# One of four weight sums is added up by an accumulating DMA instead of VectorE

## The chip, the core and the metric

The kernel runs on one core of a Trainium2 chip. The metric is the device time of one execution in microseconds (us). Its engines are TensorE (PE in the profile; PEld is its weight load), VectorE (DVE), ScalarE (ACT), GpSimd (POOL) and SyncE (SP, which here only issues DMAs).

## The reference

Two transformer layers over 512 frames of 1024 features, all in float32. The first mixes by multi-head latent attention with a chunk mask, the second by chunked attention with a learned relative bias. Each is followed by the same feed-forward network with its own weights, 1024 to 2816 to 1024, with norms before and behind:

```python
def swiglu(h, w_gate, w_up, w_down):
    return (jax.nn.silu(h @ w_gate) * (h @ w_up)) @ w_down
...
h = rms_norm(x, ffn_pre_g[layer])
f = swiglu(h, ffn_w_gate[layer], ffn_w_up[layer], ffn_w_down[layer])
x = x + rms_norm(f, ffn_post_g[layer])
```

The change lies in `h @ w_gate` and `h @ w_up` of both layers.

## The kernel before

Features lie on the partitions, frames on the free dimension. A float32 product is made of three products of rounded pieces: each operand is split into a high piece (a rounding copy on ACT, L141) and a low piece (what is left, a subtraction on DVE, L142), and high x high, high x low and low x high are added up in PSUM. So each weight tile of 128 x 1024 is loaded by SP (`raw`), cast on ACT (`whi`), subtracted on DVE (`wlo`), and then used by PE.

The hidden layer has 22 blocks of 128. The first four are computed whole. The other 18 are computed in 9 pairs per layer by `products`: the weights of a pair (gate and up of two blocks, with the input features in two halves) are cut into quarters, and seven products of half the size take the place of eight, in the manner of Strassen and Winograd. For that, sums of weight quarters are needed, and sums of input quarters, which `blocks_of` makes once per layer (`t`, with pieces `th` and `tl`, L1016 to L1019, partly on POOL). In each pair PE runs the products 0 to 6 one after the other, 24 multiplications of 256 columns a product (L1053), in the banks `be`, `al`, `ga`. Between them DVE and ACT take partial results out of the banks (`gt`, `ut`, L1057 to L1072), and at the end of a pair DVE and ACT form the gated hidden block and its pieces (`hh`, `hl`).

The quarters of a pair are four tiles in DRAM, `src[0]` to `src[3]`, here tile(0) to tile(3). `Pair` loads them into `raw[1]`, `raw[2]`, `raw[4]` and `raw[5]` of its dictionary, and product j uses `raw[j]`:

- product 0: `raw[0]` = tile(2) + tile(3), in a tile of its own
- product 1: tile(0); product 2: tile(1)
- product 3: `raw[0]` + tile(0), written over `raw[0]`
- product 4, the fifth: tile(2) + tile(0), written over `raw[4]`
- product 5: tile(3)
- product 6: `raw[3]` + tile(1), written over it once more

All four sums are DVE instructions of one line, L171. tile(2) has a ring of two buffers of its own (`sum2`), the sum `raw[0]` has another (`sum`), and the other three quarters share a ring of four buffers (`raw`) in which later loads wait until an earlier tile has been read for the last time. All loads are issued by SP in one queue.

`Feed` walks a plan of all weight tiles: it loads ahead (up to five steps within pairs), and `split(i)` calls `sums(j)` and then splits the tile. The framework puts every engine's instructions in order ahead of time, by a priority that follows the program and by when it reckons an instruction's inputs to be ready; each engine then works its queue strictly in that order, and an instruction that waits holds up what stands behind it. In this way the sums are put well ahead of their use: the first sum of a pair stands in DVE's queue more than a pair before its product.

Of the kernel before, what the change touches and what calls it, by code (L numbers as in the profile page):

```python
# [14 lines left out]
OP = mybir.AluOpType  # L15
# [53 lines left out]
def trunk(ctx: ExitStack, tc: tile.TileContext, a, out):  # L69
    nc = tc.nc  # L70
# [11 lines left out]
    def name_(n):  # L82
        uid[0] += 1
        return f"{n}_{uid[0]}"
# [63 lines left out]
    class Pair:  # L148

        def __init__(self, src):
            self.src, self.raw = src, {}

# [13 lines left out]
        def sums(self, j):  # L169
            def plus(t, x, y):  # L170
                V.tensor_tensor(t, x, y, op=OP.add)  # L171

            r = self.raw
            if j == 0:
                r[0] = r[3] = r[6] = wide[0].tile([P, 1024], F32, tag="sum", name=name_("raw"), bufs=2)
                plus(r[0], r[4], r[5])
            elif j in (3, 6):
                plus(r[j], r[j], r[j // 3])
            elif j == 4:
                plus(r[4], r[4], r[1])  # L180

    wide = [None]

# [198 lines left out]
    class Head:  # L382
# [3 lines left out]
        def __init__(self, qk, bt, scale, pv, sums):  # L386
            self.qk, self.bt, self.scale, self.pv, self.sums = qk, bt, scale, pv, sums
            self.p, self.pt = {}, None
# [493 lines left out]
    def start_a(h):  # L882
# [12 lines left out]
        def pv(pth, ptl):  # L895
            fill.until("v")
            o = bank()
            v_ = slice(h * VD, (h + 1) * VD)
            for kt in range(NQT):
                q_ = slice(kt * P, S)  # L900
                mm3(o[:, q_], (va[kt][:, 0, v_], va[kt][:, 1, v_]), (pth[:, kt, q_], ptl[:, kt, q_]),
                    kt == 0, kt == NQT - 1)
            V.reciprocal(sums, sums)
            of = U(name="of")
            nc.scalar.copy(of, o)

            def rest():
                V.tensor_tensor(of, of, spread(sums), op=OP.mult)
                oh, ol = U(F32R, "oh"), U(F32R, "ol")
                split(oh, ol, of)  # L910
                osp.append((oh, ol))

            return rest
# [415 lines left out]
```

## Time and profile before

| what | value |
|---|---|
| time, median of 3 runs | 1172.71 us |
| the three runs | 1174.03, 1170.98, 1172.71 us |
| the profiled execution: time | 1172.07 us |
| the profiled execution: span from first to last instruction | 1170.3 us |
| mean granted TensorE clock over the span | 0.992 |
| the seven products, first layer | about 237 to 428 us from the span's start |
| the seven products, second layer | about 847 to 1038 us |

A row of a timeline gives the start in us from the span's start, the length in us, the engine, the line, the operation and its operands (out<-in, buffer numbers left out), how many instructions were merged into the row, and in brackets how long the engine sat idle before it and what ended that. A row of the chain of waits gives start, length and what: an instruction of an engine, a DMA in flight, or "issue", in which the engine waited for nothing that the profile shows. Lengths on an engine can overlap by some 0.1 us, so the cost of one instruction in a full queue is better read from start to start.

### The profile page before, as it was taken

The numbers are of one execution on the slowest core, as the hardware profiler recorded it, in microseconds if no ns is written. First come the engines' busy times: TensorE is split into PE (matmuls) and PEld (weight loads), VectorE is DVE, ScalarE is ACT, GpSimd is POOL, SyncE is SP. The second block draws the span as 40 slices with busy tenths as digits, with TensorE's granted clock in tenths as the row PEclk, the third lists the DMA queues.
The fourth block names the chain that finished last, engine by engine and source line by source line (L and its number), as shares of the span: only waits on it lengthen the run. The fifth ranks groups of instructions, "written<-read, shape, count | busy, mean of one in ns | idle before, by whom it ended". The sixth has DMA issues, their size and how long they took to land.

```text
span 1170.3 us, 18693 instructions
## 1 busy us (share of the span) xinstructions
PE 1142.9 (98%) x7195; PEld 1023.0 (87%) x7195; DVE 832.5 (71%) x1405; ACT 611.4 (52%) x1151; POOL 45.6 (4%) x67
## 2 busy tenths in 40 slices
PE   9999999989999999999999999999989999999996
PEld 6888889889999998889788887789889999998886
DVE  7787648889889862236968877749899898952233
ACT  6476546556556552234436766656555565642220
POOL 0200000110000000000100000000300000000002
PEclk9999999989999999999999999999999999999998
DMA  7433144222323243233546656454123233252222
GB/s 215 118 105 91 37 163 153 99 73 91 127 90 106 85 141 129 93 113 100 179 145 156 172 150 171 118 198 142 57 91 114 85 94 123 73 175 95 99 63 73
DMA packets 53161, 137.71 MB, mean 118 GB/s; under 512 B 7184, under 2 KB 10768, under 8 KB 53072
## 3 DMA queue, kind: packets, MB, share of 16 engines
q1 hardware_dynamic: 52928, 136.47, 37.5%
q8 instruction: 57, 0.93, 0.3%
q14 instruction: 32, 0.26, 0.1%
q10 hardware_dynamic: 144, 0.04, 0.0%
HBM read 113.22 MB, written 8.59 MB: 104 GB/s over the span
## 4 chain that ended last, share of the span: by engine, by line
PE 76%; DVE 13%; DMA 4%; issue 3%; ACT 2%; POOL 1%; SPq 0%; DVEq 0%; ACTq 0%; POOLq 0%
PE b L258 16%; PE b L259 16%; PE b L260 16%; PE al L1053 12%; PE be L1053 6%; DVE wlo L142 5%; PE ga L1053 3%; DMA raw<-in_w_pair 2%; PE pt L410 2%; DVE raw L171 2%; DVE tl L142 1%; PE sc L1170 1%; PE b L1179 1%; PE bc L371 1%; PE b L1178 1%
## 5 line engine op out<-in xcount | busy, mean ns | idle before, releaser
L141 ACT CAST whi<-raw 128x1024 fp32r<-128x1024 f32 (+4 forms) x240 | 240.5, 1002 | 324.8 <-PE b L259 172.4
L142 DVE TENSOR_TENSOR wlo<-raw,whi 128x1024 fp32r<-128x1024 f32 (+4 forms) x240 | 279.8, 1168 | 167.5 <-ACT whi L141 162.2
L258 PE MATMUL b<-hh,whi 128*128 128x512 f32 (+1 forms) x364 | 136.0, 374 | 0.0
L259 PE MATMUL b<-hl,whi 128*128 128x512 f32 (+1 forms) x364 | 135.7, 373 | 0.0
L260 PE MATMUL b<-hh,wlo 128*128 128x512 f32 (+1 forms) x364 | 135.6, 373 | 0.0
L1053 PE MATMUL al<-th,whi 128*128 128x256 f32 x432 | 124.5, 288 | 2.8 <-DVE ut L1065 2.6
L1053 PE MATMUL al<-tl,whi 128*128 128x256 f32 x432 | 122.1, 283 | 0.0
L1053 PE MATMUL al<-th,wlo 128*128 128x256 f32 x432 | 122.1, 283 | 0.0
L258 PE MATMUL b<-xh,whi 128*128 128x512 f32 (+1 forms) x304 | 115.8, 383 | 1.5 <-ACT xh L145 1.5
L259 PE MATMUL b<-xl,whi 128*128 128x512 f32 (+1 forms) x304 | 113.0, 372 | 0.0
L260 PE MATMUL b<-xh,wlo 128*128 128x512 f32 (+1 forms) x304 | 112.8, 371 | 0.0
L171 DVE TENSOR_TENSOR raw<-raw,raw 128x1024 f32<-128x1024 f32 x72 | 88.1, 1225 | 24.1 <-DMA raw<-in_w_pair 23.6
L1053 PEld LDWEIGHTS al<-th,whi 128*128 128x128 f32 x432 | 82.6, 191 | 5.8 <-DVE ut L1065 4.2
L1053 PEld LDWEIGHTS al<-tl,whi 128*128 128x128 f32 x432 | 82.7, 192 | 0.0
L1053 PEld LDWEIGHTS al<-th,wlo 128*128 128x128 f32 x432 | 82.7, 191 | 0.0
L258 PEld LDWEIGHTS b<-hh,whi 128*128 128x128 f32 x364 | 68.5, 188 | 12.1
L260 PEld LDWEIGHTS b<-hh,wlo 128*128 128x128 f32 x364 | 68.5, 188 | 11.9
L259 PEld LDWEIGHTS b<-hl,whi 128*128 128x128 f32 x364 | 68.5, 188 | 11.9
L398 ACT ACTIVATE p<-p,mn 128x128 f32<-128x128 f32 (+1 forms) x96 | 54.0, 563 | 34.8 <-DVE mn L396 34.2
L328 DVE TENSOR_TENSOR acc<-acc,sq 128x256 f32<-128x256 f32 (+1 forms) x89 | 43.7, 504 | 35.1 <-ACT sq L327 33.1
L142 DVE TENSOR_TENSOR ptl<-pt,pth 128x128 fp32r<-128x128 f32 (+1 forms) x96 | 46.4, 485 | 28.6 <-ACT pth L141 21.9
L258 PEld LDWEIGHTS b<-xh,whi 128*128 128x128 f32 x304 | 57.5, 190 | 9.7 <-ACT xh L145 2.8
(265 smaller groups left out, 2852.7 us busy)
## 6 DMA issues: line engine op xcount, KB each, us to landing
raw<-in_w_pair SPq DMA_DIRECT2D x72, 512.0 KB, 3.6
raw<-in_w_down SPq DMA_DIRECT2D x38, 512.0 KB, 3.4
raw<-in_w_o SPq DMA_DIRECT2D x16, 512.0 KB, 3.6
raw<-in_w_gu SPq DMA_DIRECT2D x16, 512.0 KB, 4.3
raw<-in_w_qkb SPq DMA_DIRECT2D x16, 512.0 KB, 3.9
x<-in_x SPq DMA_DIRECT2D x16, 256.0 KB, 5.9
mid<-x SPq DMA_DIRECT2D x16, 256.0 KB, 2.2
x<-mid SPq DMA_DIRECT2D x16, 256.0 KB, 6.0
```

The lines of the kernel that those rows point to most:

```text
L141: return (nc.scalar.copy(dst_hi, src), V.tensor_tensor(dst_lo, src, dst_hi.bitcast(F32), op=OP.subtract))
L142: V.tensor_tensor(dst_lo, src, dst_hi.bitcast(F32), op=OP.subtract))
L171: V.tensor_tensor(t, x, y, op=OP.add)
L258: nc.tensor.matmul(o, l[0], r[0], start=start, stop=False)
L259: nc.tensor.matmul(o, l[0], r[1], start=False, stop=False)
L260: nc.tensor.matmul(o, l[1], r[0], start=False, stop=stop)
L328: V.tensor_tensor(self.acc[:, c], self.acc[:, c], q[:, c], op=OP.add)
L371: nc.tensor.transpose(b[:, (first + i) * P:(first + i + 1) * P], col[:, i:i + 1].to_broadcast([P, P]), ident)
L398: nc.scalar.activation(p[:, :n], p[:, :n], AF.Exp, bias=mn[:, :1], scale=-1.0, accum_out=self.sums[:, qt:qt + 1])
L410: nc.tensor.transpose(t[:, kt * P:(kt + 1) * P], p[:, kt * P:(kt + 1) * P], ident)
L1053: nc.tensor.matmul(o, l[c], r[d], start=first_ and n == 0, stop=k == K2 - 1 and n == 2, skip_group_check=True)
L1170: nc.tensor.matmul(o, q1[:, e, q_], k1[:, e, :n], start=True, stop=False)
```

## The change

`sums(0)` still adds tile(2) and tile(3) on VectorE. Behind that it issues a DMA on POOL's queue that reads tile(0) from DRAM again and adds it to `raw[4]`, the tile in which tile(2) lies. The VectorE sum for product 4 goes. The sums for products 0, 3 and 6 stay, and tile(0) is still loaded into `raw[1]`. What casts `raw[4]` for product 4 now waits for that DMA. A blank line is added above, so that the line of the sums becomes L172; lines from L181 on keep their numbers.

```diff
@@ -150,6 +150,7 @@
+
         def __init__(self, src):
             self.src, self.raw = src, {}
...
             if j == 0:
                 r[0] = r[3] = r[6] = wide[0].tile([P, 1024], F32, tag="sum", name=name_("raw"), bufs=2)
                 plus(r[0], r[4], r[5])
+                nc.gpsimd.dma_start(r[4], self.src[0], accum_op=OP.add)
             elif j in (3, 6):
                 plus(r[j], r[j], r[j // 3])
-            elif j == 4:
-                plus(r[4], r[4], r[1])
```

## The prediction

> **What bounds the kernel now.** I read the page first, then the product stage by stretches, then the chain of waits inside it, then the engines' timelines around one turn of that chain. On the page, the busy shares and the one group that the change touches:
>
> ```profile
> span 1170.3 us, 18693 instructions
> PE 1142.9 (98%) x7195; PEld 1023.0 (87%) x7195; DVE 832.5 (71%) x1405; ACT 611.4 (52%) x1151; POOL 45.6 (4%) x67
> L171 DVE TENSOR_TENSOR raw<-raw,raw 128x1024 f32<-128x1024 f32 x72 | 88.1, 1225 | 24.1 <-DMA raw<-in_w_pair 23.6
> ```
>
> TensorE is busy nearly all the time, so removed VectorE time counts only where TensorE waits for VectorE. The 72 sums of weight quarters (four in each of 18 pairs) take 88.1 us of VectorE, and VectorE stood idle 23.6 us before some of them until a load had landed. The stretches (columns: length, then busy time of PE, PEld, DVE, ACT, POOL, granted clock, DMA share, GB/s) show where that matters:
>
> ```profile
> 237.00:264.00 27.00, 23.86 (x171) 22.95 (x170) 24.00 (x31) 14.36 (x24) 2.42 (x2) 0.87 0.24 79
> 305.00:367.00 62.00, 61.01 (x501) 60.11 (x500) 54.76 (x70) 35.19 (x57) 0.00 (x0) 1.00 0.32 103
> 847.00:873.00 26.00, 22.57 (x171) 21.83 (x171) 24.04 (x31) 14.26 (x24) 2.43 (x2) 0.93 0.25 82
> 873.00:934.00 61.00, 61.00 (x507) 60.70 (x506) 54.06 (x69) 35.58 (x57) 0.00 (x0) 1.00 0.33 104
> 934.00:1018.00 84.00, 82.21 (x674) 80.99 (x673) 74.09 (x95) 47.09 (x76) 0.00 (x0) 1.00 0.30 95
> ```
>
> From 873 to 934 TensorE is never idle; from 305 to 367 and from 934 to 1018 it is. The chain of waits (start, length, what) says how long a pair of hidden blocks takes in either regime:
>
> ```profile
> 272.96 8.79 PE al L1053 x72
> ...
> 293.27 8.79 PE al L1053 x72
> 302.05 2.90 PE be L1053 x24
> ...
> 364.72 1.32 PE be L1053 x11
> 931.31 5.76 PE be L1053 x48
> ...
> 968.53 4.36 DMA raw<-in_w_pair
> ...
> 989.55 4.50 DMA raw<-in_w_pair
> ...
> 1015.33 4.68 PE be L1053 x39
> ```
>
> Where TensorE is the bound, a pair takes 293.27 - 272.96 = 20.31 us. From the seventh product at 302.05 to that at 364.72 there are three pairs: 62.67 us, 1.74 more than 3 x 20.31. From 931.31 to 1015.33 there are four: 84.02 us, 2.78 more than 81.24. In these stretches the chain leaves TensorE and turns in a loop of VectorE work and one load, 989.55 - 968.53 = 21.02 us a turn. One turn on VectorE's timeline, what TensorE's product line waited for in the whole run (us, times), and in the last row what the sums' line waited for:
>
> ```profile
> 965.50 0.74 DVE L1061 TENSOR_TENSOR gt<-gt,ga 128x256 f32<-128x256 f32 x2
> 966.16 1.22 DVE L171 TENSOR_TENSOR raw<-raw,raw 128x1024 f32<-128x1024 f32 x1
> 967.29 2.35 DVE L142 TENSOR_TENSOR wlo<-raw,whi 128x1024 fp32r<-128x1024 f32 x2
> 969.56 0.74 DVE L1065 TENSOR_TENSOR ut<-al,ut 128x256 f32<-128x256 f32 x2
> 973.02 1.23 DVE L171 TENSOR_TENSOR raw<-raw,raw 128x1024 f32<-128x1024 f32 x1 [2.71 <-DMA raw<-in_w_pair]
>   DVE tl L142: 12.3, 8
>   DVE ut L1065: 6.8, 12
>   DMA raw<-in_w_pair: 23.6, 14
> ```
>
> By the buffers the instructions name, 966.16 is the fifth product's sum (of the next pair), 967.29 holds the wlo of the sixth and of the seventh product. The sixth one's wlo frees the buffer of quarter tile(3); the load into it starts at 968.53, right behind its end; it lands 4.4 us later; and the sum at 973.02, the first product's of the pair after next, stands in VectorE's queue until then. All of VectorE's later work of the pair queues behind that sum, and so `ut` (L1065), which empties the bank that the sixth product wants, comes late: that is TensorE's wait in these pairs, (1.74 + 2.78) / 7 = 0.65 us on average. The 14 waits for the load are 7 turns in each layer. At 0.71 over TensorE's pace 7 turns would lose 5.0 us, and 2.26 per layer were lost: VectorE has a head start of about 2.7 us, which is used up first.
>
> **Part 1: the 18 fifth-product sums leave VectorE.** Its busy time falls by 18 x 1.22 = 22 us. Most of that buys nothing, because TensorE sets the time in most pairs. In the loop, start to start, the sum costs 967.29 - 966.16 = 1.13 us, and it lies directly ahead of the wlo that starts the load. Without it a turn takes 21.02 - 1.13 = 19.89 us, 0.42 under TensorE's 20.31. So the loop no longer binds, and the excess goes: 1.74 + 2.78 = 4.52 us. What is late next is TensorE itself. The gain can't exceed these two terms by much: the other fifth-product sums lie in pairs where TensorE never waits, or at the start of the stage, where TensorE waits for other work (part 4).
>
> **Part 2: 18 accumulating DMAs on POOL's queue.** Each waits for the first product's sum (it overwrites the tile this reads) and re-reads 512 KB, 9.4 MB in all, while tile(0) is still loaded for the second product and for the fourth one's sum. SP's queue loses and gains nothing. The rows of its cover:
>
> ```profile
> 952.00 1.23 DVE L171 TENSOR_TENSOR raw<-raw,raw 128x1024 f32<-128x1024 f32 x1 [2.81 <-DMA raw<-in_w_pair]
> 982.99 1.06 ACT L141 CAST whi<-raw 128x1024 fp32r<-128x1024 f32 x1
> DMA to landing us min/median/max: 3.5/3.9/4.4
> q1 hardware_dynamic: 2160, 7.87, 29.0%
> ...
> raw<-in_w_pair SPq DMA_DIRECT2D x14, 512.0 KB, 4.3
> raw<-in_w_down SPq DMA_DIRECT2D x2, 512.0 KB, 3.5
> ```
>
> The tile whose first sum ends at 953.2 is cast for the fifth product at 982.99, so 29.8 us lie between. No accumulate is in the trace. From below it takes 3.5 us, the quickest plain load; from above three slow loads' time, for two reads and a write one behind the other, 13.2 us, and with the longest POOL operation below (1.72) 14.9. I take 3.9 plus about 1 for POOL, since the bytes from HBM are a plain load's. Either end is half the cover or less, so it costs nothing. If the cover were gone, ACT's cast would wait, and behind it in ACT's queue the copies that empty the `al` and `be` banks; then TensorE waits microsecond for microsecond.
>
> **Part 3: the DMA engines.** The loads from 934 to 1018 keep the engines 29.0% of 84 us busy, 24.4 us for 16 loads, 1.5 each. An accumulate adds that once to twice. The load of the loop starts at 989.55, 15.3 us after the sum at 973.02 has ended at 974.25, so even the upper end lets it alone. Between 0 and 1.5 us on the loop per pair, I take 0. A load of tile(0) beside it may come later; with its early sum gone nothing needs it for over 10 us.
>
> **Part 4: POOL's queue at the start of the products.** POOL stands at 0.00 in the stretches above, but while the blocks are formed it works:
>
> ```profile
> 227.54 1.72 POOL L1017 TENSOR_TENSOR t<-xg,xg 128x256 f32<-128x256 f32 x1
> 229.22 0.92 POOL L1016 TENSOR_TENSOR t<-xg 128x256 f32<-128x256 f32 x1
> 230.90 0.92 POOL L1017 TENSOR_TENSOR t<-xg,xg 128x256 f32<-128x256 f32 x1 [0.76 <-ACT xg L1014]
> 233.52 0.74 POOL L1016 TENSOR_TENSOR t<-xg 128x256 f32<-128x256 f32 x1 [1.70 <-ACT xg L1014]
> 229.46 1.76 DVE L142 TENSOR_TENSOR wlo<-raw,whi 128x1024 fp32r<-128x1024 f32 x1
> 242.71 1.21 DVE L171 TENSOR_TENSOR raw<-raw,raw 128x1024 f32<-128x1024 f32 x1
> ```
>
> The second pair's first sum ends near 228.5, so its DMA enters this queue, with `t` and, through `tl`, TensorE's first products behind it (the 12.3 us above). It costs nothing if the 0.76 and 1.70 us of idle time take it up, and 1.72 per layer if it is as long as the longest POOL row and all of it shows. I take 0: about 1 us fits into the gaps. The fifth-product sum that leaves from 242.71 is behind the `tl` that TensorE waits for, so it gains nothing either.
>
> **Part 5: VectorE beside POOL.** The wlo at 229.46 took 1.76 us instead of 1.22 while POOL worked. If the writing of descriptors did the same, each accumulate would cost VectorE 0.54 us; from below 0, since an extra instruction elsewhere can't shorten one. I take 0. Even 0.54 makes the loop 20.43, only 0.12 over TensorE; over seven turns that is 0.8, which the head start of 2.7 bears. The Trainium skill (SBUF — State Buffer, Who interferes with whom) states that a VectorE instruction with two SBUF inputs contends with a GpSimd instruction that reads SBUF, and infers that descriptor generation, which writes, does not hit such an instruction. The trace agrees with the first half (1.76 against 1.22); the second no run here shows. By either reading the sum stays -4.5.
>
> **The sum.** 1172.07 (the profiled execution; its span is 1170.28, and the 1.8 outside stays) - 4.52 = 1167.55. The runs' median, 1172.71, is 0.64 above that execution, which would give 1168.2. I say 1168.
>
> **The rivals.**
> Only idle time moves: the sum at 973.02 waits 1.13 us longer, and all stays at 1172. For it: VectorE already idles 2.71 us there. Against: the load starts 0.01 us after the wlo's end, so it moves up with it. It would be right if the buffer were freed by something other than this wlo.
>
> The start of the products pays. TensorE's wait there is followed by a slower clock: 0.87 over 27 us and 0.93 over 26, that is 3.5 and 1.8 us lost for much the same wait. If POOL's issue shows with 1.72 us in one layer and stretches the slow time by such a 1.7, 3.4 come back: 1171.0, and 1174.4 if in both layers.
>
> VectorE is held up while POOL makes descriptors, instead of merely slowed. With 1.72 us per accumulate a turn takes 21.61, 1.30 over TensorE. Over the head start, 7 x 1.30 - 2.7 = 6.4 us per layer are lost: 1167.6 + 12.8 = 1180. It decides from 1.13 us on, where the turn is back at 21.02. For it: 1.76 against 1.22 shows that the two engines do meet. Against: that row shows 0.54, and beside an operation that reads two operands.
>
> The program's order changes: the sum that waits for the load is put ahead of `ut`. A pair at TensorE's pace gives the price:
>
> ```profile
> 274.80 1.22 DVE L142 TENSOR_TENSOR wlo<-raw,whi 128x1024 fp32r<-128x1024 f32 x1
> ```
>
> This wlo would start at 273.67 without the sum, the load land 1.22 + 4.4 later at 279.3, the sum end at 280.5 and the first `ut` at 280.9, while TensorE wants the bank two thirds into the stretch of `al`, at 272.96 + 5.9 = 278.9: 2 us in each of 14 pairs, 28 us, 1196. Against: `ut` stands ahead of it in every pair shown.
>
> The accumulate runs so long that it meets the loop's load, 15.3 us after its own start. By the 1.5 us of engine time in part 3 a turn takes 21.4, and 7 x 1.08 - 2.7 = 4.9 us per layer are lost: 1177. Against: the upper end, 14.9. The Trainium skill (DMA: Bandwidth & Descriptors, Issuing engines are not separate DMA queues) says that DMAs issued from all engines run on the same 16 DMA engines and interleave; by that rule the two would share as soon as they overlap. No row here shows two large queues that do.
>
> **How the numbers follow.** Forecast 0.61, only idle time moves 0.10, the start pays 0.13, VectorE held up 0.08, the order 0.05, the shared engines 0.03. A measurement of this kernel tells about 0.3%, 3.5 us, from no change, and 4.5 is only 1 us beyond it. The slow clock after TensorE's wait alone differs by 1.7 us between the two layers, so of the forecast's 0.61 I count 0.48 as faster and 0.13 as within 0.3%. Of the start's 0.13, 0.02 is still faster, 0.10 within and 0.01 slower. Faster 0.48 + 0.02 = 0.50, same 0.13 + 0.10 + 0.10 = 0.33, slower 0.01 + 0.08 + 0.05 + 0.03 = 0.17. The forecast's own range is 1165.8 to 1169.3 (1.7 about it). The range asked for reaches up over the idle-time case and the start's to 1174.5 and down to 1165; the three dear cases, 0.16 together, stay outside.
>
> **What would show it.** L171's group falls to 54 sums; 18 DMAs stand on POOL with a queue of their own; pairs take 20.31 us between 302 and 364 and between 931 and 1011; the 6.8 us before `al` from `ut` are all but gone; the sum's wait for its load is no longer in the chain. Wrong would be: turns still near 21 us, a cast that waits for the accumulate, a wlo of over 1.22 us beside it, or a longer wait for `tl` at the start of the products.

## The result and the profile after

The changed kernel takes 1184.05 us (median of 6 runs, 1181.66 to 1186.87) against 1172.14 for the kernel before (6 runs, 1170.98 to 1174.03): the ratio is 1.0101, with a 95% interval of 1.0082 to 1.0119. It is slower by 1%, where 1168 was forecast and 1165 to 1174.5 given as the range. The profiled execution took 1182.32 us with a span of 1180.5, 10.25 us over the profiled execution of before.

From the page of the changed kernel: busy shares, queues, the sums' group, and the DMA issues of the pairs (count, size, median us from issue to landing):

```profile
PE 1145.6 (97%) x7195; PEld 1024.5 (87%) x7195; DVE 819.3 (69%) x1387; ACT 613.7 (52%) x1151; POOL 63.8 (5%) x85
q1 hardware_dynamic: 52928, 136.47, 36.9%
q0 software_dynamic: 2592, 9.44, 4.9%
L172 DVE TENSOR_TENSOR raw<-raw,raw 128x1024 f32<-128x1024 f32 x54 | 66.2, 1227 | 16.9 <-DMA raw<-in_w_pair 16.3
raw<-in_w_pair SPq DMA_DIRECT2D x72, 512.0 KB, 3.6
raw<-in_w_pair POOLq DMA_DIRECT2D x18, 512.0 KB, 5.5
```

The change does what it says. The sums are 54 instead of 72 and their time fell by 22 us, and VectorE even waits less for loads ahead of them (16.3 us, before 23.6). 18 accumulating DMAs have a queue of their own and land 5.5 us after their issue. The plain loads of the pairs land as fast as before. So the loss has to be sought where TensorE waits. What TensorE's product line waited for in the changed kernel (us, times), and its stretches from the second to the seventh pair of each layer (columns as in the prediction):

```profile
  DVE ut L1065: 21.7, 22
  DVE tl L142: 13.0, 8
264.00:394.00 130.00, 123.69 (x1013) 121.87 (x1012) 106.88 (x135) 72.04 (x115) 5.20 (x6) 1.00 0.46 125
881.00:1008.00 127.00, 123.56 (x1012) 121.74 (x1011) 106.31 (x134) 72.08 (x115) 5.20 (x6) 1.00 0.47 127
```

The waits for `ut` were to go; they rose from 6.8 to 21.7 us (matmuls and weight loads together). The chain of waits of the changed kernel says what one such pair looks like:

```profile
294.20 1.55 issue
295.75 1.06 ACT whi L141
...
296.84 1.24 DVE wlo L142
...
298.09 4.34 DMA raw<-in_w_pair
...
303.70 0.43 DVE ut L1065
...
304.17 1.69 PE al L1053 x12
305.86 5.64 PE be L1053 x47
```

and VectorE's timeline in the same pair shows why:

```profile
299.72 1.23 DVE L142 TENSOR_TENSOR wlo<-raw,whi 128x1024 fp32r<-128x1024 f32 x1 [1.65 <-ACT whi L141]
300.86 0.42 DVE L1065 TENSOR_TENSOR ut<-al,ut 128x256 f32<-128x256 f32 x1
302.56 1.23 DVE L172 TENSOR_TENSOR raw<-raw,raw 128x1024 f32<-128x1024 f32 x1 [1.28 <-DMA raw<-in_w_pair]
303.70 0.42 DVE L1065 TENSOR_TENSOR ut<-al,ut 128x256 f32<-128x256 f32 x1
```

Before, both `ut` stood together and the sum that waits for its load came behind them. Now that sum stands between the two. The second `ut` could follow the first by 1.45 us, the multiplications of one block (20.31 / 14), but waits for a load that it does not use and for a sum of the pair after next. TensorE wants the bank that this `ut` empties for the second block of the sixth product, and stands still.

In numbers, from the starts of the multiplications in the trace: the second to the seventh pair take 129.67 us in the first layer and 126.79 in the second, where 6 x 20.31 = 121.86 is TensorE's own pace. That is 12.74 us of waits, against 4.52 before: 8.2 of the 10.25. The first pair of each layer is longer by 0.43 and 2.19 us, 2.6 more. The rest of the span is 0.6 shorter.

### The profile page after: what moved, and what is told of

It is laid out like the page before. It is cut to its first block, busy times and chain, and to the rows that moved or that the text cites. A ratio compares the mean times of both kernels' runs of the same rounds, so it can differ in the third digit from the quotient of the medians.

```text
span 1180.5 us, 18739 instructions
## 1 busy us (share of the span) xinstructions
PE 1145.6 (97%) x7195; PEld 1024.5 (87%) x7195; DVE 819.3 (69%) x1387; ACT 613.7 (52%) x1151; POOL 63.8 (5%) x85
## 3 DMA queue, kind: packets, MB, share of 16 engines
q1 hardware_dynamic: 52928, 136.47, 36.9%
q0 software_dynamic: 2592, 9.44, 4.9%
## 4 chain that ended last, share of the span: by engine, by line
PE 77%; DVE 9%; DMA 6%; issue 4%; ACT 2%; POOL 1%; SPq 0%; DVEq 0%; ACTq 0%; POOLq 0%
PE b L258 16%; PE b L259 16%; PE b L260 16%; PE al L1053 9%; PE be L1053 8%; DMA raw<-in_w_pair 5%; DVE wlo L142 3%; PE ga L1053 2%; PE pt L410 2%; ACT whi L141 2%; DVE tl L142 1%; PE b L1179 1%; PE sc L1170 1%; PE b L1178 1%; POOL r L354 1%
## 5 line engine op out<-in xcount | busy, mean ns | idle before, releaser
L1053 PE MATMUL al<-th,whi 128*128 128x256 f32 x432 | 125.3, 290 | 9.7 <-DVE ut L1065 9.5
L1053 PE MATMUL al<-tl,whi 128*128 128x256 f32 x432 | 122.1, 283 | 0.0
L1053 PE MATMUL al<-th,wlo 128*128 128x256 f32 x432 | 122.0, 283 | 0.0
L1053 PEld LDWEIGHTS al<-th,whi 128*128 128x128 f32 x432 | 82.5, 191 | 14.0 <-DVE ut L1065 12.2
L1053 PEld LDWEIGHTS al<-th,wlo 128*128 128x128 f32 x432 | 82.7, 191 | 0.0
L1053 PEld LDWEIGHTS al<-tl,whi 128*128 128x128 f32 x432 | 82.6, 191 | 0.0
L172 DVE TENSOR_TENSOR raw<-raw,raw 128x1024 f32<-128x1024 f32 x54 | 66.2, 1227 | 16.9 <-DMA raw<-in_w_pair 16.3
L260 PEld LDWEIGHTS b<-xh,wlo 128*128 128x128 f32 x304 | 57.4, 189 | 8.9
```

Source lines behind the costliest of these rows:

```text
L260: nc.tensor.matmul(o, l[1], r[0], start=False, stop=stop)
L1053: nc.tensor.matmul(o, l[c], r[d], start=first_ and n == 0, stop=k == K2 - 1 and n == 2, skip_group_check=True)
```

## The experiments

Theory Q is that the order in VectorE's queue made the loss, and not the DMA. Each kernel ran beside the kernel before on one chip, and its ratio is to that one. The experiments ran on three chips, on which the kernel before took 1171.1 to 1171.7 us, and 1172.1 beside the changed kernel. So times of different experiments can be off by 1 us against each other, and there the ratios are what to compare.

**Fixed order.** The first sum of every pair but the first two of a layer is put behind the second `ut` of two pairs earlier, with the accumulating DMA kept. (The added lines shift the products' line from L1053 to L1058 and the sums' to L173.)

```diff
-                plus(r[0], r[4], r[5])
+                with ExitStack() as st:
+                    if self.q % 9 >= 2:
+                        st.enter_context(tc.issue_after(pins[self.q - 2].ins))
+                    plus(r[0], r[4], r[5])
                 nc.gpsimd.dma_start(r[4], self.src[0], accum_op=OP.add)
...
-                        V.tensor_tensor(u[:, A1], o, u[:, A1], op=OP.add)
+                        m_ = V.tensor_tensor(u[:, A1], o, u[:, A1], op=OP.add)
+                        if e:
+                            pins.append(m_)
```

> The changed kernel, with one order fixed: the first product's sum stays behind both ut additions (L1065 of before) of two pairs earlier, as it stood before the change. Theory Q (queue order: the sum that waits for its load slipped in ahead of the second ut): the 12.8 us that TensorE waits at the sixth product go, pairs take 20.31 us, and with the old 4.5 us gone too the time is near 1168, 4 to 5 below before. Rival D (the accumulating DMA costs by itself: its packets and its issue stretch the loads and slow VectorE): the order does not matter, the time stays at 1180 to 1184. Rival C (the slower clock at the start of the products, 2.6 us more in the changed kernel): 1170 to 1171, the pairs at 20.31 but the first pair of each layer still at 27 us or more.

Measured: 1168.84 us (1167.84 to 1171.03, 12 runs), ratio 0.9980 (0.9971 to 0.9989). The instructions are those of the changed kernel. By the names in the two traces VectorE's order differs in the second `ut` of 12 pairs alone, TensorE's in one multiplication of the seventh product in each of these pairs (it stood ahead of the sixth product's second block and no longer does), and that of the other engines not at all. With that, 1.2% of the time is gone (1.0101 to 0.9980), some 14 us. The stretches, the chain, and all that the product line waited for in this kernel:

```profile
264.00:386.00 122.00, 122.00 (x1011) 121.39 (x1011) 106.33 (x134) 72.48 (x114) 5.21 (x6) 1.00 0.46 131
872.00:993.00 121.00, 121.00 (x1003) 120.40 (x1002) 104.63 (x131) 71.75 (x114) 5.21 (x6) 1.00 0.46 130
273.09 8.79 PE al L1058 x72
...
293.40 8.79 PE al L1058 x72
  DVE tl L142: 13.7, 8
  ACT th L141: 3.8, 8
  DVE gt L999: 0.2, 1
```

TensorE is never idle there, a pair takes 293.40 - 273.09 = 20.31 us, and no wait for `ut` is left. With the same six DMAs in a stretch on POOL (5.21 us busy) and the same DMA share of 0.46 as in the changed kernel, rival D has fallen. Rival C holds in part: the first pair of each layer still takes 26.9 us, together 1.6 more than before. And 0.9980 is 2.3 us below before, less than the 4 to 5 expected; the runs below say where the rest stays.

**Without the DMA.** The changed kernel, its accumulating DMA left out.

```diff
-                nc.gpsimd.dma_start(r[4], self.src[0], accum_op=OP.add)
```

> The changed kernel without the accumulating DMA: the fifth product then uses tile(2) alone, so that term of the sum is left out. Theory Q: the sum's removal alone makes the framework put the first product's sum ahead of the second ut, so TensorE still waits at the sixth product by some 1 us in six pairs per layer, 1180 to 1184. Rival D: without the DMA no cost is left, 1168.

Measured: 1181.66 us (1179.92 to 1184.47), ratio 1.0092 (1.0076 to 1.0108). VectorE's timeline of this kernel:

```profile
299.06 0.42 DVE L1064 TENSOR_TENSOR ut<-al,ut 128x256 f32<-128x256 f32 x1
300.73 1.23 DVE L172 TENSOR_TENSOR raw<-raw,raw 128x1024 f32<-128x1024 f32 x1 [1.25 <-DMA raw<-in_w_pair]
301.87 0.42 DVE L1064 TENSOR_TENSOR ut<-al,ut 128x256 f32<-128x256 f32 x1
  DVE ut L1064: 27.4, 24
```

By the names in the two traces TensorE, VectorE, ScalarE and SyncE work in exactly the order of the changed kernel; only POOL's 18 DMAs are missing. Taking a sum away is enough to move another one between the `ut`, and with it comes nearly all of the loss.

**Without the DMA, order fixed.** Both edits together.

> Without the accumulating DMA (that term left out), and with the order fixed behind both ut. Theory Q: 1167 to 1168, and within 1 us of the kernel with the order fixed and the DMA, so that the DMA is free. Rival D: 1168 here, but 12 us or more below the kernel with the order fixed and the DMA.

Measured: 1166.20 us (1165.65 to 1167.87), ratio 0.9962 (0.9949 to 0.9975). The order is worth 15.5 us here (1.3%), about what it is worth with the DMA (1.2%). But the DMA is not free to within 1 us: 1168.84 - 1166.20 = 2.6 on the same chip. Between the two kernels without a fixed order the ratios are 1.0101 and 1.0092, about 1 us apart, and their intervals overlap.

**No DMA for the first two pairs of a layer.** With the order fixed and the DMA kept, but for these two pairs the sum stays on VectorE. No DMA is then issued while the blocks are formed.

```diff
-                nc.gpsimd.dma_start(r[4], self.src[0], accum_op=OP.add)
+                if self.q % 9 >= 2:
+                    nc.gpsimd.dma_start(r[4], self.src[0], accum_op=OP.add)
...
+            elif j == 4 and self.q % 9 < 2:
+                plus(r[4], r[4], r[1])
```

> The kernel with the order fixed behind both ut and the accumulating DMA, but in the first two pairs of each layer the fifth product's sum stays on VectorE, so that no DMA is issued on POOL while the blocks are formed. Theory S: TensorE's waits at the start of the products are back at 4.4 us, 1.7 us less over both layers than with all 18 DMAs (1168.8): 1167. Rival T (the rest of the DMA's cost is spread over the pairs or is the slower clock's chance): 1168 to 1169.

Measured: 1167.12 us (1165.60 to 1171.11, 12 runs), ratio 0.9961 (0.9947 to 0.9974), against 0.9980 with all 18: some 2 us less. The two intervals just overlap (0.9974 and 0.9971), so the times alone would not settle it. The timelines of POOL and VectorE do, first with all 18 DMAs (order fixed), then with the 14:

```profile
227.37 1.72 POOL L1022 TENSOR_TENSOR t<-xg,xg 128x256 f32<-128x256 f32 x1
229.04 0.93 POOL L182 DMA_DIRECT2D raw<-in_w_pair  x1
229.70 1.05 POOL L1021 TENSOR_TENSOR t<-xg 128x256 f32<-128x256 f32 x1
230.73 1.70 POOL L1022 TENSOR_TENSOR t<-xg,xg 128x256 f32<-128x256 f32 x1
229.30 2.54 DVE L142 TENSOR_TENSOR wlo<-raw,whi 128x1024 fp32r<-128x1024 f32 x1
231.76 0.96 DVE L1024 SCALAR_TENSOR_TENSOR t<-t,xg 128x256 f32<-128x256 f32 x1
```

```profile
227.51 1.72 POOL L1025 TENSOR_TENSOR t<-xg,xg 128x256 f32<-128x256 f32 x1
229.19 0.92 POOL L1024 TENSOR_TENSOR t<-xg 128x256 f32<-128x256 f32 x1
230.87 0.92 POOL L1025 TENSOR_TENSOR t<-xg,xg 128x256 f32<-128x256 f32 x1 [0.76 <-ACT xg L1022]
229.44 1.76 DVE L142 TENSOR_TENSOR wlo<-raw,whi 128x1024 fp32r<-128x1024 f32 x1
231.12 0.96 DVE L1027 SCALAR_TENSOR_TENSOR t<-t,xg 128x256 f32<-128x256 f32 x1
  DVE tl L142: 12.0, 8
  ACT th L141: 1.9, 4
```

The issue takes 0.93 us in the middle of the block sums, and POOL's next two sums end 0.78 us later relative to the first one. With no gap left between them, POOL's sums run beside the wlo for longer, and the wlo takes 2.54 us instead of 1.76. The block that VectorE works on next (`t`, L1024 or L1027) comes 0.78 us later too, and the pieces that TensorE's first product waits for are made from it. By the starts of its multiplications, TensorE's waits at the start of the products are 5.1 to 5.2 us per layer in the four kernels with all 18 DMAs and 4.2 to 4.4 in those with none there. The list at the end of the fence, against 13.7 and 3.8 us in the kernel with the order fixed and all 18, says the same.

**Late sums, no DMA.** The kernel before, its first sums moved still further back: behind the last bank read of two pairs earlier (L1069 of before) instead of `ut`. The lines in `sums` are those of the fixed order.

```diff
-                        V.tensor_tensor(t[:, A1], t[:, A1], o, op=OP.add)
+                        m_ = V.tensor_tensor(t[:, A1], t[:, A1], o, op=OP.add)
+                        if e:
+                            pins.append(m_)
```

> The kernel before, all four sums on VectorE, with one order fixed: the first product's sum stands behind the last bank read (L1069) of two pairs earlier, some 5 us later in the queue than before, where its load has landed. Theory Q (the loop of 21.02 us exists only because this sum stands in the queue ahead of its load): VectorE no longer idles 2.7 us there, its work is 18.3 us in a pair of 20.31, the 4.5 us of waits go, 1167 to 1168 with no DMA at all. Rival W (VectorE's amount of work is what bounds those pairs): the pairs stay near 21 us, 1171 to 1173.

Measured: 1166.51 us (1165.87 to 1168.62), ratio 0.9965 (0.9952 to 0.9978). From its profile, the sums' group and two turns of the chain of waits, which lies on TensorE alone there:

```profile
L172 DVE TENSOR_TENSOR raw<-raw,raw 128x1024 f32<-128x1024 f32 x72 | 88.2, 1225 | 1.4 <-DMA raw<-in_w_pair 0.8
271.73 8.79 PE al L1058 x72
...
292.04 8.79 PE al L1058 x72
```

All 72 sums are still on VectorE, but it waits 0.8 us for loads ahead of them instead of 23.6, and every pair but the first of a layer keeps TensorE's pace (292.04 - 271.73 = 20.31). By the names in the traces TensorE's order is that of the kernel before; some other instructions of VectorE and ScalarE moved a little with the sums. What bound the slow pairs before was the place of one instruction and not the amount of work, so rival W has fallen. This is the version to keep: 4 to 5 us below before, with no DMA on POOL.

**Late sums with the DMA**, for all pairs and for all but the first two:

> The changed kernel with the first product's sum moved behind the last bank read of two pairs earlier, as in the kernel with late sums and no DMA (1166.5). Theory S (what the DMA still costs lies at the start of the products, where its issue on POOL stands ahead of the block sums: TensorE's waits there were 5.2 us per layer with the DMA and 4.4 without): 1168 to 1169, as with the order fixed behind both ut, 1.7 above the late kernel without the DMA. Rival E (the DMA helps once nothing is in its way, by VectorE's 22 us): below 1166.

> Late sums, and the accumulating DMA in all but the first two pairs of each layer. Theory S: as the late kernel without a DMA, 1166 to 1167, since TensorE bounds every pair at 20.31 us in both. Rival E: 1165 or less.

Measured: 1169.09 us (ratio 0.9982, 0.9971 to 0.9992) and 1167.57 us (0.9965, 0.9952 to 0.9977). Once no pair waits, the DMA has nothing left to give. With all 18 it costs some 2 us against the late sums alone (0.9982 against 0.9965, their intervals overlap), and with 14 the two can't be told apart. Rival E has fallen.

**The order alone.** The kernel before, all four sums on VectorE, with the first sum forced between the two `ut` in pairs 1 to 6 (counted from 0) of each layer; to that end it is issued from within the pair two earlier.

```diff
-                        V.tensor_tensor(u[:, A1], o, u[:, A1], op=OP.add)
+                        with ExitStack() as st_:
+                            if e and 1 <= p < pairs - 2:
+                                st_.enter_context(tc.issue_after(feed.early().ins))
+                            V.tensor_tensor(u[:, A1], o, u[:, A1], op=OP.add)
```

> The kernel before, all four sums on VectorE and no DMA on POOL, with one order forced: in six pairs of each layer the first product's sum of two pairs later stands between the two ut additions, as in the changed kernel. Other instructions may move a little with it. Theory Q: TensorE waits at the second block of the sixth product in those pairs, 1 us or more in each, and the time is 1180 or more, with nothing of the change in the kernel. Rival R (the place between the ut costs only where the fifth product's sum is gone): within 3 us of before.

Measured: 1176.03 us (1175.12 to 1176.50), ratio 1.0039 (1.0027 to 1.0051). It slows the kernel with nothing of the change in it, so rival R is wrong, but by 4.3 us (1176.03 - 1171.71) and not by the 8 or more that I expected. The reason is in the starts of the multiplications: in every other pair the framework also moved other instructions, and TensorE waits there 0.1 to 0.8 us instead of 1.0 to 1.4. As a clean price of the order this run is spoilt by these moves; the fixed order gives that price.

**Ahead of both.** The changed kernel with the first sum forced ahead of both `ut` (`if not e and ...` in the edit above).

> The changed kernel, its first product's sum (of two pairs later) forced ahead of both ut additions instead of the second alone, in pairs 1 to 6 of each layer. Theory Q, worked out from the changed kernel's rows: the wlo of the sixth product ends at 298.1, the load lands 4.4 later, the sum ends at 303.7 and the first ut at 304.1, where TensorE wants its bank at 286.99 + 14.4 = 301.4, so 2.7 us in each of some 12 pairs instead of 1.1: 32 us over the 1168.8 of the order behind both, 1195 to 1201. Rival H (the changed kernel's extra time is not this wait but something that comes with the new program as a whole): near 1184.

Measured: 1182.02 us (1181.01 to 1183.39), ratio 1.0090 (1.0066 to 1.0114). It is no dearer than the changed kernel, against what I had worked out. VectorE's timeline is as expected; TensorE's is not:

```profile
343.45 1.23 DVE L172 TENSOR_TENSOR raw<-raw,raw 128x1024 f32<-128x1024 f32 x1 [1.74 <-DMA raw<-in_w_pair]
344.60 0.75 DVE L1076 TENSOR_TENSOR ut<-al,ut 128x256 f32<-128x256 f32 x2
342.32 0.28 PE L1061 MATMUL be<-xh,whi 128*128 128x256 f32 x1
...
343.88 0.28 PE L1061 MATMUL be<-xl,whi 128*128 128x256 f32 x1
345.07 0.39 PE L1061 MATMUL al<-th,whi 128*128 128x256 f32 x1 [0.92 <-DVE ut L1076]
```

The framework also moved 14 multiplications of the seventh product (into `be`) ahead of the sixth (into `al`), and 13 to 15 in most of the other pairs. They fill 1.7 us of the wait, and some 1.1 are left of the 2.7 that I had reckoned. Its time does not separate Q from H; the wait for `ut` in its rows is Q's.

## Why the prediction was wrong

**The step that failed** is the tacit one that the order of VectorE's queue stays as it was. It stood in the list as the fourth rival, "the sum that waits for the load is put ahead of `ut`", at 0.05, with "`ut` stands ahead of it in every pair shown" as the argument against. That row says nothing of a program with one instruction less: the kernel without the sum and without the DMA has the new order too. In place of the 4.5 us that were to go, TensorE waits 12.74 us for the second `ut`. With the order put back and all 18 DMAs kept, the kernel is 2.3 us faster than before where 4.5 was forecast, and most of what is missing is part 4's. That the sum slips in because its load is now reckoned to land before the second `ut` is ready fits with what moved, but it is only argued; no run shows the framework's reckoning.

**The rival's price** was 2 us in 14 pairs, 28 us. It came to 1.06 us on average in 12 pairs (0.35 to 2.70), 12.74 in all, since the sum passed the second `ut` alone, which is wanted 1.45 us later than the first, and the first pair of each layer kept its order. Less the old 4.52 that is 8.2 us. The loop before turned six times a layer as well, and not seven: of the 14 waits for a load, two (at 227 and 837 us) lie ahead of the products. The head start of 2.7 us is then 2.0 (6 x 0.71 - 2.26).

**Part 1** was right as a mechanism: with the order kept, the turn no longer binds, and pairs take 20.31 us. Its 4.5 us is borne out by the kernel with neither sum nor DMA (0.9962, that is 4.5 of 1172) and by the late sums (0.9965). It took the loop for a matter of work, though, and the late sums show that the work could have stayed.

**Parts 2 and 3** held. The accumulate takes 5.5 us to landing (5.4 to 6.8; I took 4.9), far below the cover of 29.8, and no cast waits for it. The plain loads of the pairs land in 3.6 us, as before.

**Part 5** held inside the pairs, and not where the blocks are formed. VectorE beside POOL's issue in the changed kernel, first in a pair, then the wlo that meets an issue at the start of the products:

```profile
282.55 1.22 DVE L142 TENSOR_TENSOR wlo<-raw,whi 128x1024 fp32r<-128x1024 f32 x1
282.90 0.88 POOL L178 DMA_DIRECT2D raw<-in_w_pair  x1 [20.48 <-DVE ut L1065]
228.85 2.55 DVE L142 TENSOR_TENSOR wlo<-raw,whi 128x1024 fp32r<-128x1024 f32 x1
```

The first wlo keeps its 1.22 us, and 16 of the 18 sums and wlo that meet an issue take at most 1.23: the 0.54 of the range did not come there. The other two, one in each layer, took 2.55 and 2.53 us, where the same wlo took 1.76 before. The prediction had named a wlo of over 1.22 us as a sign of being wrong. POOL's block sums run beside these two as well, and no run separates the issue's own share from theirs. The Trainium skill (SBUF — State Buffer, Who interferes with whom) infers that the making of descriptors does not hit such an instruction. The 16 agree with that, and the two leave it open.

**Part 4** was sized too low. I took 0 of a range up to 1.72 us per layer; TensorE's waits grew by 0.8 per layer, through the slower block sums and that wlo; the longer wait for `tl` that the prediction named as a sign of being wrong is there. In all, the 18 DMAs cost 2.6 us with the order fixed and some 2 with late sums, of which 1.5 to 2.2 go when the first two pairs keep their sum on VectorE. What the rest is, the runs leave open; it is no more than the spread of single runs.

## What to carry to other kernels

In a queue that is worked strictly in order, an instruction that waits for a load is paid for by whatever stands behind it, so its place matters more than its length: moving 14 sums 3 to 5 us back gave what the removal of 18 of them was meant to give. Where a framework orders the instructions, the removal of one can reorder the others; predict with the order as an unknown, and fix by an explicit edge what must not move. When a smaller amount of work makes a kernel slower, look for the same instruction with another neighbour in the two timelines.

## What the hardware showed

An accumulating DMA of 512 KB took 5.5 us from issue to landing against 3.6 for a plain load, and some 0.87 us of POOL. By the two queues' rows, 9.44 MB took 4.9% of the DMA engines' time and 136.47 MB (all other loads, and the stores) took 36.9%: an accumulated byte occupied the DMA engines 1.9 times as long as one of the other queue. Where an issue stood between POOL's sums, the VectorE subtraction beside them took 2.55 us instead of 1.76; beside an issue alone it kept its 1.22.
